# A fifth buffer for the split weights and one more half of lookahead in a decoder trunk on one core

## The chip, the core and the metric

The kernel runs on one core of a Trainium2 chip. The core has five engines, each with its own instruction queue that is worked off in order: TensorE (PE in the rows; its weight loads are PEld), VectorE (DVE), ScalarE (ACT), GpSimd (POOL) and SyncE (SP), which here issues nearly all the loads. The metric is the device time of one execution in microseconds; before the change it is 2073.59 us, the median of three runs.

## The reference

One sequence of 256 tokens with 2048 features goes through two layers in float32. Layer 0 mixes tokens by pooling, layer 1 by attention; each layer then has a gated feed-forward part (FFN) with 5632 inner features. A vector c gives every layer six modulation vectors.

```python
cond = silu(c)
for i in range(2):
    mod = cond @ w_ada[i] + b_ada[i]                  # 2048 -> 6 x 2048
    sh1, sc1, g1, sh2, sc2, g2 = split(mod, 6)
    h = rmsnorm(x, norm_g[i, 0]) * (1 + sc1) + sh1
    y = pool_mixer(h, pool_w, pool_scale) if i == 0 else moba_attention(h, w_qkv, w_o, rel_table)
    x = x + g1 * y
    h = rmsnorm(x, norm_g[i, 1]) * (1 + sc2) + sh2
    u = causal_conv3(h @ w_up[i], conv_w[i]) + conv_b[i]   # 2048 -> 2 x 5632
    val, gate = split(u, 2)
    x = x + g2 * ((silu(gate) * val) @ w_down[i])          # 5632 -> 2048
return rmsnorm(x, final_g)
```

With 256 tokens the attention has a single block, so every head attends causally to its own block with the relative bias. All weights are read once.

## The kernel before

**Split weights.** Activations lie feature by feature: 128 features on the partitions, 256 tokens along the row. Each float32 operand is split in two parts, hi (rounded to fp32r) and lo (the rest), and each product is made of three matmuls: hi x hi, hi x lo and lo x hi. The weights are used in *pieces* (`steps`) of 512 x 512, 1 MB, loaded by SyncE into one of five raw tiles (`RAW = 5`), in order. `w_use` (line 986) takes a piece in two *halves* of 128 x 1024: ScalarE copies the half to hi, VectorE subtracts hi from the raw half and writes lo. Both parts have a ring of `HB = 4` tiles of their own.

**Lookahead.** A half that is split is put on `pending`; only when more than `LAG = 2` halves wait there does `run_half` emit the matmuls of the oldest. So in program order the split of half n is followed by the matmuls of half n-2 and then by what belongs to it: the hooks of its piece (scores, norms), one or two entries of `tasks` (convolution, SiLU, residual additions), at most two `folds` and the `deferred` work. ScalarE and VectorE work in order, so a later split stands behind all this.

**Stages.** The *opening* computes modulation vectors of layer 0 out of w_ada in slices (tiles ws, sums accs, rows row on TensorE, columns mods), and the pooling mixer beside them; its loads are paced by raw tiles that come free. Then come FFN 0 (pieces uv, ug for w_up, d for w_down), attention (pieces k, q, v, wo; scores sc, softmax tiles sm) and FFN 1. The modulation of layer 1 is summed on VectorE beside the matmuls (tiles wa, sum acc, an accumulation of 128 x 2048 a time), and folded into columns by transposes (turn, cols). These accumulations are events of their own between two pieces (`ada_side`) and are not tied to `run_half`.

**What sets the order.** Up to event 200 (pieces up to about 90) a list scheduler orders each engine by its own estimate of times and the priorities in the code; from there on program order holds. The opening's first actions are the loads of c and x, the squares of x (sqx, into raw tiles), transposes of x to xT, and `cond` = SiLU(c) on ScalarE, before the first weight slice is used.

**Memory.** The pool lays its tiles one after another in SBUF: five raw tiles of 8192 bytes a partition, then four hi tiles, then four lo tiles. Each hi or lo tile is 1056 words long, of which words 16 to 1039 are used. `ones` is 128 x 128, of which column 0 is read (`slice_use`); `rel` holds the bias table.

Of the kernel before, what the change touches and what calls it, by code (L numbers as in the profile page):

```python
# [9 lines left out]
F32 = mybir.dt.float32  # L10
F32R = mybir.dt.float32r
# [6 lines left out]
P = 128  # L18
# [3 lines left out]
BUCKETS = 32  # L22
# [3 lines left out]
def bucket_starts():  # L26

    exact = BUCKETS // 2

    def bucket(n):  # L30
        if n < exact:
            return n
        big = exact + int(math.log(n / exact) / math.log(MAX_DIST / exact) * (BUCKETS - exact) + 1e-9)
        return min(big, BUCKETS - 1)

    of = [bucket(n) for n in range(4 * MAX_DIST)]
    return [next((n for n, b in enumerate(of) if b >= want), 1 << 20) for want in range(BUCKETS)]
# [19 lines left out]
def trunk(ctx: ExitStack, tc: tile.TileContext, x, c, norm_g, w_ada, b_ada, pool_w, pool_scale, w_qkv, w_o,  # L57
          rel_table, w_up, conv_w, conv_b, w_down, final_g, out):
    nc = tc.nc
    pe, ve, ac = (InOrder(tc, e) for e in (nc.tensor, nc.vector, nc.scalar))  # L60
    _, S, D = x.shape
# [4 lines left out]
    H = rel_table.shape[1]  # L66
    NT = S // P
    SCALE = float(P) ** -0.5
    C = 512
    S2 = 2 * S  # L70
    Q = 32

    const = ctx.enter_context(tc.tile_pool(name="const", bufs=1))
    wp = ctx.enter_context(tc.tile_pool(name="wp", bufs=1))
# [2 lines left out]
    dram = ctx.enter_context(tc.tile_pool(name="dram", bufs=1, space=bass.MemoryType.DRAM))  # L77

    PE_BLOCKS = ((2, 5, 8, 11, 14), (3, 7, 11, 15), (2, 4, 6, 9, 11, 13, 15), (2, 5, 7, 10, 13, 15), ())
    RAW, HB, LAG, T4, PRIO = 5, 4, 2, 6, 1000  # L80

    def raw_tile(name):
        return wp.tile([P, 4 * C], F32, tag="raw", name=name, bufs=RAW)
# [4 lines left out]
    def aux(name):  # L88
        return psum.tile([P, C], F32, tag="aux", name=name, bufs=2)

    def wt(shape, tag, bufs, name, dt=F32):
        return work.tile(shape, dt, tag=tag, bufs=bufs, name=name)


    ident = const.tile([P, P], F32, name="ident")
    make_identity(nc, ident)
    ones = const.tile([P, P], F32, name="ones")
    nc.gpsimd.memset(ones, 1.0)
    same = const.tile([P, P], F32, name="same")
    for q in range(4):  # L100
# [565 lines left out]
    def bias_rows():  # L666

        starts = bucket_starts() + [1 << 20]
        st = const.tile([P, BUCKETS + 1], F32, name="starts")
        for b, v in enumerate(starts):  # L670
            nc.gpsimd.memset(st[:, b:b + 1], float(v))
        rel = const.tile([BUCKETS, H + 8], F32, name="rel")[:, :H]
        nc.gpsimd.dma_start(rel, rel_table)
        e = wt([H, S + P], "t4", T4, "bias_e")
        nc.gpsimd.memset(e, NEG)
        for t in range(NT):
            ni = wt([P, 1], "st", 8, f"ni{t}", I32)
            nc.gpsimd.iota(ni, pattern=[[0, 1]], base=t * P, channel_multiplier=1)
            n = wt([P, 1], "st", 8, f"nf{t}")
            ve.tensor_copy(n, ni)  # L680
            ge = wt([P, BUCKETS + 1], "oh", 2, f"ge{t}")
            ve.tensor_scalar(ge, st, n, None, op0=ALU.is_le)
            oh = wt([P, BUCKETS + 1], "oh", 2, f"oh{t}")
            ve.tensor_tensor(oh[:, :BUCKETS], ge[:, :BUCKETS], ge[:, 1:], op=ALU.subtract)
            ps = aux(f"ohp{t}")
            pe.transpose(ps[:BUCKETS, :P], oh[:, :BUCKETS], ident)
            ohT = wt([BUCKETS, P], "vec", 4, f"ohT{t}")
            ve.tensor_copy(ohT, ps[:BUCKETS, :P])
            ps2 = aux(f"ohe{t}")
            pe.matmul(ps2[:H, :P], rel, ohT, start=True, stop=True)  # L690
            ve.tensor_copy(e[:, P - 1 + t * P:P - 1 + (t + 1) * P], ps2[:H, :P])
        nc.gpsimd.dma_start(bias_dram, e)
# [273 lines left out]
    def run_half():  # L966
        i, half, hi, lo = pending.pop(0)
        steps[i][3](half, hi, lo)
        if half == 1:
            for f in hooks.get(i, ()):  # L970
                f()
        h_next = ahead.pop(0) if ahead else None
        if h_next:
            h_next()
        else:
            run_tasks(2 if len(tasks) > MANY else 1)
        for _ in range(2):
            if folds:
                folds.pop(0)()
        for d in list(deferred):  # L980
            d[0] -= 1
            if d[0] <= 0:
                deferred.remove(d)
                d[1]()

    def w_use(i):
        def use(r):
            for half in range(2):

                hi, lo = (wp.tile([P, 2 * C + 32], F32R, tag=w, name=f"{w}{i}_{half}", bufs=HB)[:, 16:16 + 2 * C]  # L990
                          for w in ("hi", "lo"))
                src = r[:, half * 2 * C:(half + 1) * 2 * C]
                ac.activation(hi, src, AF.Copy)
                ve.tensor_tensor(lo, src, hi.bitcast(F32), op=ALU.subtract)
                pending.append((i, half) + tuple(t.rearrange("p (k c) -> p k c", k=2) for t in (hi, lo)))
                if len(pending) > LAG:
                    run_half()
        return use
# [47 lines left out]
    i = 0  # L1046
    for s in range(4):
        nxt = slices[s + 1] if s < 3 else []
        for g in range(FIRST):
            event(w_load(i), w_use(i))  # L1050
            i += 1
            if g == 0:
                at(len(events) - 1, lambda s=s: (slice_done(3, s, s > 0), h_blocks(0, 1, 4 * s, 4)))
            while nxt and (FIRST - SPARE) * (8 - len(nxt)) < 8 * (g + 1):
                event(*nxt.pop(0))
# [3 lines left out]
    while i < len(steps):  # L1059
        event(w_load(i), w_use(i))  # L1060
        i += 1
        if side:
            due = min(due + rates[steps[i - 1][0].tensor.name] + (LATE if side[0][:2] == (1, 5) else 0), 2.0)
        quiet = any(-PRE <= i - e < QUIET for e in ends) or i < START
        while side and due >= 1.0 and not quiet:
            due -= 1.0
            p = side.pop(0)
            event(ada_load(*p), ada_side(*p))
# [64 lines left out]
```

## Time and profile before

| | us |
|---|---|
| runs | 2073.27, 2073.59, 2078.25 |
| median of the runs | 2073.59 |
| the profiled execution | 2076.08 |
| its span | 2074.3 |
| TensorE busy in it | 2013.0 (97%) |
| VectorE busy | 1641.4 (79%) |
| ScalarE busy | 960.2 (46%) |

The span reaches from the first to the last instruction of the profiled execution; the rows further down are of that execution. A row of a timeline merges equal instructions that follow each other; the bracket at its end is the engine's idle time ahead of it and what ended it. TensorE's matmuls overlap, so a matmul's own duration is more than the time from its start to the next one's.

### The profile page before, as it was taken

Reading aid. Unit: us, or ns where it says so; the run is one execution under the profiler, and the core shown is the slowest. Engines: PE = TensorE matmul, PEld = TensorE weight load, DVE = VectorE, ACT = ScalarE, POOL = GpSimd, SP = SyncE. Lnnn points to the kernel's source line nnn. Section 1 sums busy time; section 2 is a strip of 40 time slices with the busy share of each in tenths; the row PEclk is TensorE's granted clock in tenths of the full one; section 3 lists DMA queues with packets and bytes.
Section 4 is the critical chain, followed back from the end, with each engine's and each line's share of the span. In section 5 each row is a group of like instructions: output and inputs, shape, how many; then the busy total and the mean of one; then the engine's idle time right before and its main releaser. Section 6 shows DMA issues by size and latency. Waiting matters only on the chain. (4 is left out here: it accounts for less than half of the span.)

```text
span 2074.3 us, 38497 instructions
## 1 busy us (share of the span) xinstructions
PE 2013.0 (97%) x16292; PEld 1907.9 (92%) x16292; DVE 1641.4 (79%) x2023; ACT 960.2 (46%) x1206; POOL 12.0 (1%) x64
## 2 busy tenths in 40 slices
PE   6898999999999999999999999999999999999998
PEld 2445999999999999999989889999999999999998
DVE  6887899899889999997787887879885666556666
ACT  3112534566454345444444444446543555435454
POOL 1000000000000000000000000000000000000000
PEclk8988999999999999999999999999999999999999
DMA  9998999655997989896888788678875555556551
GB/s 355 346 363 324 345 346 326 222 191 196 336 360 279 377 320 320 305 324 213 311 288 326 265 308 313 223 250 284 280 268 187 200 195 192 197 189 200 187 202 62
DMA packets 236445, 558.78 MB, mean 269 GB/s; under 512 B 9272, under 2 KB 9592, under 8 KB 221680
## 3 DMA queue, kind: packets, MB, share of 16 engines
q1 hardware_dynamic: 234800, 553.17, 75.4%
q8 instruction: 127, 2.08, 0.4%
q0 software_dynamic: 896, 2.49, 0.3%
q10 hardware_dynamic: 576, 0.67, 0.1%
q14 instruction: 46, 0.38, 0.0%
HBM read 554.17 MB, written 2.12 MB: 268 GB/s over the span
## 5 line engine op out<-in xcount | busy, mean ns | idle before, releaser
L50 DVE TENSOR_TENSOR lo<-w,hi 128x1024 fp32r<-128x1024 f32 x656 | 790.9, 1221 | 260.0 <-ACT hi L50 259.1
L50 ACT ACTIVATE hi<-w 128x1024 fp32r<-128x1024 f32 x656 | 683.2, 1059 | 630.5 <-PE d L50 185.6
L50 PE MATMUL uv<-h,hi 128*128 128x256 f32 x2816 | 485.1, 278 | 3.8 <-ACT h L50 3.8
L50 PE MATMUL d<-act,hi 128*128 128x256 f32 x2816 | 482.0, 277 | 0.6 <-ACT hi L50 0.6
L50 PE MATMUL ug<-h,hi 128*128 128x256 f32 x2816 | 481.8, 276 | 0.0
L50 PEld LDWEIGHTS uv<-h,hi 128*128 128x128 f32 x2816 | 426.6, 189 | 4.5 <-ACT h L50 4.1
L50 PEld LDWEIGHTS d<-act,hi 128*128 128x128 f32 x2816 | 424.9, 188 | 0.9 <-ACT hi L50 0.8
L50 PEld LDWEIGHTS ug<-h,hi 128*128 128x128 f32 x2816 | 424.0, 188 | 0.0
L50 PE MATMUL d<-act,lo 128*128 128x256 f32 x1408 | 387.4, 277 | 4.0 <-DVE lo L50 4.0
L50 PE MATMUL uv<-h,lo 128*128 128x256 f32 x1408 | 387.9, 277 | 0.0
L50 PE MATMUL ug<-h,lo 128*128 128x256 f32 x1408 | 386.3, 276 | 0.0
L50 PEld LDWEIGHTS d<-act,lo 128*128 128x128 f32 x1408 | 263.9, 188 | 4.8 <-DVE lo L50 4.8
L50 PEld LDWEIGHTS uv<-h,lo 128*128 128x128 f32 x1408 | 265.1, 189 | 0.0
L50 PEld LDWEIGHTS ug<-h,lo 128*128 128x128 f32 x1408 | 263.5, 188 | 0.0
L50 DVE SCALAR_TENSOR_TENSOR acc<-wa,cond,acc 128x2048 f32<-128x2048 f32 x105 | 246.3, 2346 | 6.6 <-DMA wa<-in_w_ada_dram 6.3
L50 DVE SCALAR_TENSOR_TENSOR accs<-ws,cond,accs 128x512 f32<-128x512 f32 (+1 forms) x179 | 157.4, 882 | 17.2 <-ACT accs L50 7.9
L50 PE MATMUL k<-h,hi 128*128 128x256 f32 x512 | 93.7, 285 | 1.1 <-ACT h L50 1.1
L50 PE MATMUL row<-ws,cond 128*1 128x512 f32 x152 | 81.5, 663 | 8.3 <-DMA ws<-in_w_ada_dram 8.3
L50 PE MATMUL q<-h,hi 128*128 128x256 f32 x512 | 88.7, 278 | 0.0
L50 PE MATMUL wo<-o,hi 128*128 128x256 f32 x512 | 88.3, 277 | 0.0
L50 PEld LDWEIGHTS k<-h,hi 128*128 128x128 f32 x512 | 80.1, 191 | 2.3 <-ACT h L50 1.4
L50 PE MATMUL v<-hi,h 128*128 128x512 f32 x256 | 80.1, 394 | 0.0
(157 smaller groups left out, 1753.9 us busy)
## 6 DMA issues: line engine op xcount, KB each, us to landing
w<-in_w_up_dram SPq DMA_DIRECT2D x176, 1024.0 KB, 5.1
wa<-in_w_ada_dram SPq DMA_DIRECT2D x112, 1024.0 KB, 5.8
w<-in_w_down_dram SPq DMA_DIRECT2D x88, 1024.0 KB, 5.1
ws<-in_w_ada_dram SPq DMA_DIRECT2D x56, 1024.0 KB, 7.6
w<-in_w_qkv_dram SPq DMA_DIRECT2D x48, 1024.0 KB, 6.4
ws<-in_w_ada_dram SPq DMA_DIRECT2D x48, 512.0 KB, 6.5
w<-in_w_o_dram SPq DMA_DIRECT2D x16, 1024.0 KB, 6.8
pw<-in_pool_w_dram SPq DMA_DIRECT2D x4, 1024.0 KB, 9.0
```

What stands on the lines that cost most here:

```text
L50: ins = call(*args, **kwargs)
```

## The change

Each part of the split weights gets five tiles in place of four, and `LAG` goes from 2 to 3, so that the matmuls of half n are emitted behind the split of half n+3. To make room the padding of these tiles goes, `ones` shrinks to 128 x 32, and `rel` moves to another pool and loses its padding. Between the hi and the lo tiles stands a tile `gap` of 512 bytes a partition, which is cleared once. The table of thresholds takes 48 columns in place of 33, of which 33 are used.

```diff
-    RAW, HB, LAG, T4, PRIO = 5, 4, 2, 6, 1000
+    RAW, HB, LAG, T4, PRIO = 5, 5, 3, 6, 1000
...
+    rel = wt([BUCKETS, H], "rel", 1, "rel")
...
-    ones = const.tile([P, P], F32, name="ones")
+    ones = const.tile([P, Q], F32, name="ones")
...
-        st = const.tile([P, BUCKETS + 1], F32, name="starts")
+        st = const.tile([P, 48], F32, name="starts")[:, :BUCKETS + 1]
...
-        rel = const.tile([BUCKETS, H + 8], F32, name="rel")[:, :H]
...
+    gap = []
+
     def w_use(i):
         def use(r):
             for half in range(2):
-
-                hi, lo = (wp.tile([P, 2 * C + 32], F32R, tag=w, name=f"{w}{i}_{half}", bufs=HB)[:, 16:16 + 2 * C]
-                          for w in ("hi", "lo"))
+                hi = wp.tile([P, 2 * C], F32R, tag="hi", name=f"hi{i}_{half}", bufs=HB)
+                if not gap:
+
+                    gap.append(wp.tile([P, P], F32, tag="gap", name="gap", bufs=1))
+                    nc.gpsimd.memset(gap[0], 0.0)
+                lo = wp.tile([P, 2 * C], F32R, tag="lo", name=f"lo{i}_{half}", bufs=HB)
```

The order of each engine changes with it. First pair: ScalarE at the very start, before and now. bT_r are the biases that are loaded for transposing, sqx the squares of x (x_90 and x_92 before, x_91 and x_93 now), xps a transposed piece of x.

```order
L123 DMA bT_r_108<-in_b_ada_dram 96x128
L50 ACT_TABLE_LOAD
L50 ACTIVATE cond<-cT 128x16
L123 DMA bT_r_108<-in_b_ada_dram 32x128
L123 DMA bT_r_111<-in_b_ada_dram 64x128
L50 ACTIVATE sqx_118,ms_117<-x_90 128x2048
L50 ACTIVATE sqx_120,ms_117<-x_92 128x2048
L50 ACTIVATE xT<-xps_135 128x512
```

```order
L125 DMA bT_r_109<-in_b_ada_dram 96x128
L125 DMA bT_r_109<-in_b_ada_dram 32x128
L125 DMA bT_r_112<-in_b_ada_dram 64x128
L50 ACT_TABLE_LOAD
L50 ACTIVATE sqx_119,ms_118<-x_91 128x2048
L50 ACT_TABLE_LOAD
L50 ACTIVATE cond<-cT 128x16
L50 ACTIVATE sqx_121,ms_118<-x_93 128x2048
L50 ACTIVATE xT<-xps_136 128x512
```

The table load and cond stood ahead of the last two loads of biases; now all three loads come first, one square stands ahead of cond, and there is a second table load.

Second pair: VectorE in the attention, at the v piece 155 of the second group of heads, before and now. sm0_1 and sm1_1 are the softmax tiles of its two row blocks of tokens, sc1_1 scores that TensorE has just made, acc1_4 a sum of the modulation of layer 1.

```order
L50 TENSOR_TENSOR lo154_1_11285<-w154_11139,hi154_1_11284 128x1024
L50 TENSOR_TENSOR sm1_1_11300<-sc1_1_0_11301,bias1_11247 128x512
L50 TENSOR_TENSOR sm1_1_11300<-sc1_1_2_11305,bias1_11247 128x512
L50 TENSOR_REDUCE mx1_1_11309<-sm1_1_11300 128x4
L50 RECIPROCAL ri0_1_11312<-su0_1_11258 128x4
L50 TENSOR_SCALAR sm0_1_11249<-sm0_1_11249,ri0_1_11312 128x128 x4
L50 SCALAR_TENSOR_TENSOR acc1_4_10992<-wa1_4_4_11208,cond_94,acc1_4_10992 128x2048
L50 TENSOR_TENSOR lo155_0_11324<-w155_11211,hi155_0_11323 128x1024
```

```order
L50 TENSOR_TENSOR lo154_1_11271<-w154_11115,hi154_1_11270 128x1024
L50 SCALAR_TENSOR_TENSOR acc1_4_10957<-wa1_4_4_11157,cond_95,acc1_4_10957 128x2048
L50 TENSOR_TENSOR lo155_0_11296<-w155_11160,hi155_0_11295 128x1024
L50 TENSOR_TENSOR sm1_1_11311<-sc1_1_0_11312,bias1_11258 128x512
L50 TENSOR_TENSOR sm1_1_11311<-sc1_1_2_11316,bias1_11258 128x512
L50 TENSOR_REDUCE mx1_1_11320<-sm1_1_11311 128x4
L50 RECIPROCAL ri0_1_11323<-su0_1_11269 128x4
L50 TENSOR_SCALAR sm0_1_11260<-sm0_1_11260,ri0_1_11323 128x128 x4
L50 TENSOR_TENSOR lo155_1_11330<-w155_11160,hi155_1_11329 128x1024
```

The half lo155_0 stood behind the work on the scores and now stands ahead of it; the accumulation stays ahead of lo155_0.

Third pair: VectorE in FFN 0 at piece 84, the first down-projection's second part. dy0 to dy3 are results of the down-projection that wait to be added to the residual xT once their gate vector is known.

```order
L50 SCALAR_TENSOR_TENSOR xT_100<-dy0_5533,mod_113,xT_100 128x256 x4
L50 SCALAR_TENSOR_TENSOR xT_100<-dy1_5597,mod_113,xT_100 128x256 x4
L50 SCALAR_TENSOR_TENSOR xT_100<-dy2_5661,mod_113,xT_100 128x256 x4
L50 SCALAR_TENSOR_TENSOR xT_100<-dy3_5913,mod_113,xT_100 128x256 x2
L50 TENSOR_TENSOR lo84_0_6672<-w84_6525,hi84_0_6671 128x1024
```

```order
L50 SCALAR_TENSOR_TENSOR xT_101<-dy0_5544,mod_114,xT_101 128x256 x4
L50 SCALAR_TENSOR_TENSOR xT_101<-dy1_5608,mod_114,xT_101 128x256 x4
L50 SCALAR_TENSOR_TENSOR xT_101<-dy2_5672,mod_114,xT_101 128x256
L50 TENSOR_TENSOR lo84_0_6646<-w84_6500,hi84_0_6645 128x1024
L50 SCALAR_TENSOR_TENSOR xT_101<-dy2_5672,mod_114,xT_101 128x256
L50 TENSOR_TENSOR lo84_1_6678<-w84_6500,hi84_1_6677 128x1024
```

Fourteen additions stood ahead of lo84_0, now nine; both halves of the piece now stand among them.

## Rows read from the trace of the kernel before

**Rows 1.** Page, part 1: busy us, share of the span, instructions.
```profile
PE 2013.0 (97%) x16292; PEld 1907.9 (92%) x16292; DVE 1641.4 (79%) x2023; ACT 960.2 (46%) x1206; POOL 12.0 (1%) x64
```
**Rows 2.** Stretches: length, PE, PEld, DVE, ACT, POOL busy (instructions), PEclk, DMA share, GB/s.
```profile
100.00:200.00 100.00, 91.26 (x343) 44.53 (x341) 74.77 (x134) 18.88 (x30) 0.67 (x2) 0.88 0.91 337
...
1500.00:1600.00 100.00, 100.00 (x884) 100.00 (x884) 70.58 (x87) 41.78 (x42) 0.00 (x0) 1.00 0.69 237
```
**Rows 3.** Waits of PE: us in total, times, longest us.
```profile
PE d L50 <- DVE lo L50: 4.0, 3, 1.9
...
PE v L50 <- DVE lo L50: 2.5, 3, 0.8
PE k L50 <- DVE lo L50: 2.1, 4, 1.2
...
PE d L50 <- ACT hi L50: 0.6, 1, 0.6
```
**Rows 4.** Timeline of PE at 883 us: start, us, instruction, idle before.
```profile
882.80 0.39 PE L50 MATMUL d<-act,hi 128*128 128x256 f32 x2
883.02 0.28 PE L50 MATMUL d<-act,lo 128*128 128x256 f32 x1
883.14 0.39 PE L50 MATMUL d<-act,hi 128*128 128x256 f32 x2
885.40 0.46 PE L50 MATMUL d<-act,lo 128*128 128x256 f32 x1 [1.87 <-DVE lo L50]
```
**Rows 5.** Stretches with the columns of Rows 2.
```profile
885.60:889.00 3.40, 3.40 (x17) 3.40 (x17) 3.40 (x3) 0.00 (x0) 0.00 (x0) 0.50 1.01 335
...
206.00:940.00 734.00, 728.23 (x6392) 727.02 (x6391) 668.08 (x781) 364.55 (x435) 0.79 (x1) 1.00 0.85 303
...
866.00:932.00 66.00, 64.09 (x549) 63.70 (x548) 63.53 (x83) 32.91 (x37) 0.00 (x0) 0.97 0.86 306
```
**Rows 6.** Timeline of DVE in the attention's second group of heads.
```profile
1080.85 2.35 DVE L50 SCALAR_TENSOR_TENSOR acc<-wa,cond,acc 128x2048 f32<-128x2048 f32 x1
1083.11 2.36 DVE L50 TENSOR_TENSOR lo<-w,hi 128x1024 fp32r<-128x1024 f32 x2
```
**Rows 7.** Timeline of DVE around 668 us.
```profile
662.47 5.63 DVE L50 SCALAR_TENSOR_TENSOR xT<-dy,mod,xT 128x256 f32<-128x256 f32 x14
668.00 1.22 DVE L50 TENSOR_TENSOR lo<-w,hi 128x1024 fp32r<-128x1024 f32 x1
```
**Rows 8.** Timeline of ACT at the start of the program.
```profile
7.04 1.28 ACT L50 ACT_TABLE_LOAD   x1 [7.04 <-DMA x<-in_x_dram]
8.34 0.22 ACT L50 ACTIVATE cond<-cT 128x16 f32<-128x16 f32 x1
8.87 0.89 ACTq L123 DMA_DIRECT2D bT_r<-in_b_ada_dram  x2
9.80 1.91 ACT L50 ACTIVATE sqx<-x 128x2048 f32<-128x2048 f32 x1 [1.25 <-DMA x<-in_x_dram]
...
13.60 1.06 ACT L50 ACTIVATE xT<-xps 128x512 f32<-128x512 f32 x2
```
**Rows 9.** Timeline of DVE: the first accumulations over weight slices.
```profile
25.93 12.19 DVE L50 SCALAR_TENSOR_TENSOR accs<-ws,cond,accs 128x512 f32<-128x512 f32 x16 [2.19 <-ACT accs L50]
```
**Rows 10.** Waits of the SP queue: us in total, times, longest us.
```profile
SPq L251 <- DVE accs L50: 104.2, 44, 9.4
```
**Rows 11.** Stretches of 5 us with the columns of Rows 2.
```profile
25.00:30.00 5.00, 2.06 (x4) 0.17 (x4) 3.89 (x6) 2.21 (x4) 0.00 (x0) 0.88 0.76 261
30.00:35.00 5.00, 1.11 (x2) 0.00 (x0) 4.86 (x7) 0.00 (x0) 0.00 (x0) 0.50 1.05 395
```
**Rows 12.** Groups by line and shape, DVE and then ACT: count, busy us, mean ns, idle.
```profile
L50 DVE TENSOR_TENSOR lo<-w,hi 128x1024 fp32r<-128x1024 f32 x656 | 790.9, 1221 | 260.0 <-ACT hi L50 259.1
...
L50 DVE TENSOR_TENSOR val<-gate,val 128x1024 f32<-128x1024 f32 x22 | 26.9, 1224 | 3.4 <-ACT gate L50 3.0
...
L50 ACT ACTIVATE hi<-w 128x1024 fp32r<-128x1024 f32 x656 | 683.2, 1059 | 630.5 <-PE d L50 185.6 <-PE ug L50 152.3 <-PE uv L50 141.9
...
L50 ACT ACTIVATE gate<-gate 128x1024 f32<-128x1024 f32 x22 | 23.3, 1059 | 13.7 <-DVE gate L50 13.6
```

## The prediction

> **What bounds the kernel now.** I read the page first, then the engines by stretches of 100 us, then TensorE's waits, and last the timelines around the waits. TensorE is busy 97% of the span [rows 1]. From about 206 us on it runs without a pause nearly everywhere: 1500 to 1600 us holds 884 matmuls and no idle time, so one matmul starts every 113 ns, and a half of a piece (4 feature blocks x 2 row blocks x 3 products = 24 matmuls) takes 2.72 us [rows 2]. Nothing in this change shortens a matmul. The opening, up to 206 us, is another regime: the DMA engines are busy 0.91 of 100 to 200 us, TensorE issues 343 matmuls, and its mean granted clock is 0.88 [rows 2]. So the change can act in two places: on the pauses of the long part, and on the opening.
>
> **The pauses that belong to this change.** TensorE waits for a split weight half in eleven places after 206 us: d for lo 4.0 us in three waits, v for lo 2.5 us in three, k for lo 2.1 us in four, d for hi 0.6 us in one, together 9.2 us [rows 3]. Idle time undercounts a pause, because a matmul's modelled end (0.28 us after its start) lies after the start of the next. At 883 us a lo matmul normally starts 0.22 us after the pair of hi matmuls ahead of it; after the pause it starts 2.26 us after its pair, so 2.04 us were lost where 1.87 us of idle time stand [rows 4]. That is 0.17 us a wait, 1.9 us for eleven: 11.1 us. Behind that pause the clock falls from 2.4 to 1.2 GHz for 3.4 us (0.50 granted, 17 matmuls) [rows 5], which costs half of it, 1.7 us. All that the edit of the buffers could give back is therefore 12.8 us: 3.2 around 668 us (two lo waits of together 2.1 us, the one hi wait, 0.5 us of undercount), 3.7 at 883 us, 3.0 in the three v waits, 2.8 in the four k waits.
>
> **What three halves ahead removes.** In the second pair of rows in the section on the change, VectorE takes the half lo155_0 after two bias additions, a maximum, four scalings and an accumulation (acc, 2.3 us). Those additions wait for TensorE's scores, and lo stands behind all of it in order; it begins at 1083.11 us, behind an acc that begins at 1080.85 us [rows 6]. With the change the same lo stands ahead of the additions. A task of half n then follows the lo of half n+3 and not of half n+2, so TensorE has one more half, 2.72 us, before it misses the next. The three v waits cost 1.0 us each, so they go: -3.0. Of the k waits, two are behind such a chain and go; the other two are behind a row of transposes and reductions on VectorE that folds an accumulation, and I leave 0.5 us there: -2.3.
>
> The other two bursts have a VectorE that is full and not one that waits: 63.53 us busy of the 66 from 866 to 932 us [rows 5]. There a half ahead is worth less than 2.72 us, since the same work has still to be done. What VectorE has done more when the burst begins is one lo, 1.14 us from start to start [rows 6], and what moves behind the late lo is the task work that stood just ahead of it. At 883 us that is one product (val, 1.22 us): 2.3 us together. The accumulation over the next mixer's weights stays ahead of lo, as it is written at the load's place and not at the half's. So the 2.04 us go, the fall of the clock behind them probably too, but VectorE stays full to 932 us and takes some back: I take -2.3 of 3.7. At 668 us fourteen residual additions stand ahead of lo84_0 in one row of 5.63 us [rows 7]; in the new order nine do (third pair of rows). TensorE's new order also asks for that half earlier, so I take -2.0 of 3.2. Sum: -(3.0 + 2.3 + 2.3 + 2.0) = -9.6 us.
>
> The Trainium skill (Perfetto Trace Analysis, Identifying Performance Opportunities) says that consistent bubbles, the same gap over and over on the engine that should be saturated, can mean that buffers have run out. Here the gaps are few and unlike, so by that rule buffers are not short and the term would be 0; that case is among the rivals.
>
> **What the opening costs.** The change renames and moves tiles, and the scheduler orders the opening by its own estimates, so ScalarE's first rows change (first pair of rows). Now: two loads of biases are issued until 9.76 us, the table load and cond are already behind, and the squares begin at 9.80 us and lead to the first xT copy at 13.60 us, 3.80 us later [rows 8]. Before cond there was an idle engine, so its table load of 1.28 us and cond's 0.22 us delayed nothing. In the new order these stand behind the loads: table load, first square, a second table load, cond, second square. The xT copy then starts at 9.80 + 1.28 + 3.80 + 1.28 + 0.22 = 16.38 us, 2.8 us later. That has no cover. The rest of ScalarE's chain follows in order, and VectorE's first accumulation, at 25.93 us, waits for the ScalarE accumulation ahead of it [rows 9]; that accumulation frees the first weight tile, and the SyncE queue waits up to 9.4 us for it [rows 10]. The DMA engines already run dry there: 0.76 busy from 25 to 30 us, where every full stretch shows over 1.0 [rows 11]. As the opening is bound by DMA, I add all of it: +2.8 us. Bounds: 0, if a later hole swallows it; 5.6, if the shift moves as much again into a stretch of the lower clock.
>
> On the table load the Trainium skill (ScalarE: Activation LUTs, What ACT_TABLE_LOAD costs) counts a drain of 1380 ns beside the 1283 ns. In the trace cond starts 0.02 us after its table load ends, so no drain follows it [rows 8]; with the page's figure the term would be an estimated 4.2 us and the sum 1.4 us worse.
>
> **The rest.** Of the table of ones the kernel reads one column only, and the moved table rel is loaded once: 0. The memset of the gap has the shape that the ones had, whose own shrinks: 0. The parts lose their 128-byte padding. The pool lays the tiles in a row, so raw and hi tiles were 64 bytes off a multiple of 4096 and now are on it; hi and lo of one half lie 20,992 bytes apart instead of 16,896, both 512 above a multiple of 4096. A product of two tiles that lie multiples of 4096 bytes apart (gate and val) takes 1224 ns, the same shape in lo 1221; the activation in place on gate 1059 ns, hi 1059 [rows 12]. So I take no change of any duration.
>
> **Sum.** 2076.08 (the profiled execution, 1.8 above its span) - 9.6 + 2.8 = 2069.3 us. That execution lies 2.5 us above the median of the runs, 2073.59; carried over: **2066.8 us**.
>
> **Rivals.** (a) The shift of the opening is absorbed, as it has holes of its own, and the bursts clear fully: 2073.59 - 12.8 = 2060.8, or about 2063 with one of the two. For it: the DMA engines are at 0.91 between 100 and 200 us, not full. Against it: the first hole is caused by the very chain that gets longer.
> (b) VectorE is the bound in its bursts and takes back all at 668 and 883 us; only the waits on scores go: 2073.59 - 5.3 + 2.8 = 2071.1. For it: 63.53 of 66 us busy [rows 5]. By the rule of the Trainium skill above (Perfetto Trace Analysis) nothing at all goes, and the opening alone would give 2076.4; the trace agrees only in that no gap repeats on a beat. Both are no change by measurement.
> (c) Slower: the equal addresses of raw and hi make the two-input lo longer on VectorE. From 206 to 940 us VectorE is idle 734 - 668 = 66 us [rows 5], that is 0.24 us for each of 270 halves. Up to a lo of 1.46 us nothing shows; a quarter longer (+0.305 us) costs 270 x 0.065 = 17.5 us, 2084.3. Against it: the equal durations of [rows 12], where both inputs lay as raw and hi now do.
>
> **Chances.** The forecast, 2063.5 to 2069, 0.46, of which 0.36 lies below 2067.4; (a) 0.18; (b) 0.27; (c) 0.09. What counts as a change is 0.3%, 6.2 us, about what a measurement of this kernel can tell: faster below 2067.4, slower above 2079.8. Faster 0.36 + 0.18 = 0.54, same 0.10 + 0.27 = 0.37, slower 0.09. The range of 8 in 10 goes from all of (a), 2060.5, to just under the case in which the opening alone counts, 2075.5.
>
> **What would show it.** Right: no wait of v for lo, the k waits under 1 us, no stretch at the lower clock near 885 us; ScalarE's first xT copy near 16.4 us and two table loads ahead of it; the first accumulation on VectorE near 28.7 us; 113 ns between matmuls and lo at 1.22 us as now. Wrong: waits for lo in the same places, TensorE reaching its steady stretch at 206 us or before, or any duration of lo, hi or a matmul that differs.

## The result, and the profile after

The changed kernel takes 2124.38 us, the median of four runs (2121.93 to 2126.78), beside 2074.77 us for the kernel before: a ratio of 1.0237, 95% interval 1.0224 to 1.0249. It is slower by 50 us. The prediction said 2066.8 us, and its range ended at 2075.5 us.

The profiled execution is 50.3 us longer in its span (2124.6 against 2074.3 us). The page's busy times of the engines after, in us, answer [rows 1]:

```profile
PE 2068.7 (97%) x16292; PEld 1966.7 (93%) x16292; DVE 1643.4 (77%) x2023; ACT 960.3 (45%) x1207; POOL 12.1 (1%) x65
```

VectorE and ScalarE do the same work in the same time. TensorE has the same 16292 instructions and is busy 55.7 us longer. The groups by line and shape say the same of the splits (count, busy us, mean ns, idle):

```profile
L50 DVE TENSOR_TENSOR lo<-w,hi 128x1024 fp32r<-128x1024 f32 x656 | 794.2, 1222 | 319.3 <-ACT hi L50 317.6
L50 ACT ACTIVATE hi<-w 128x1024 fp32r<-128x1024 f32 x656 | 682.4, 1056 | 673.3 <-PE d L50 214.7
```

1222 and 1056 ns stand where 1221 and 1059 ns stood [rows 12]. The stretches of the changed kernel (columns of [rows 2]) show the difference:

```profile
300.00:400.00 100.00, 100.00 (x854) 100.00 (x853) 88.08 (x107) 39.26 (x44) 0.00 (x0) 1.00 0.85 296
1500.00:1600.00 100.00, 100.00 (x851) 100.00 (x850) 74.77 (x88) 45.28 (x49) 0.00 (x0) 1.00 0.70 243
```

In them TensorE waits for nothing, its granted clock is 1.00 (2.4 GHz), and it has 851 matmuls in 100 us where it had 884 [rows 2]. From start to start that is 117.8 ns on average and not 113.3. (A stretch also counts the matmuls that only reach into it, so 100 us divided by its count comes out up to 0.4 ns low.) The timeline of TensorE in the changed kernel at 1500 us (start, us, instruction) shows three matmuls at this pace:

```profile
1500.40 0.40 PE L50 MATMUL uv<-h,hi 128*128 128x256 f32 x2
1500.63 0.28 PE L50 MATMUL uv<-h,lo 128*128 128x256 f32 x1
1500.75 0.40 PE L50 MATMUL uv<-h,hi 128*128 128x256 f32 x2
```

Three matmuls take 0.35 us from start to start; in the kernel before they take 0.34 [rows 4]. The waits for the split weights are gone. Of TensorE's waits only these do not lie in the opening, and they are the norms' (us in total, times, longest; of the two of uv one ends the opening):

```profile
PE uv L50 <- ACT h L50: 3.9, 2, 2.7
...
PE rrow L50 <- DVE st_r L50: 2.6, 2, 1.3
...
PE k L50 <- ACT h L50: 1.1, 1, 1.1
```

For every matmul of 128x128 weights against 256 columns I took the time from its start to the next start, from 210 us on. Two groups stand apart: 111 to 114 ns (called **fast** from here on), and 115 to 121 ns (**slow**). The kernel before has 13,652 matmuls at the fast pace and 1,141 at the slow one, the changed kernel 88 and 14,768. So the slow pace is not new: the kernel before has it too, in short spells.

**Sum.** 13,627 more slow matmuls at 4.44 ns (100 us / 851 less 100 us / 884) are +60.5 us. The pauses, which the prediction put at 12.8 us, are gone, all of them: -12.8. The long part starts later: the 40th matmul of the FFN starts at 211.5 us and not at 208.6: +2.9. Together +50.6 us; the spans differ by 50.3.

### The profile page after: what moved, and what is told of

It reads as the page before. It is cut to its first block, busy times and chain, and to the rows that moved or that the text cites. A ratio compares the mean times of both kernels' runs of the same rounds, so it can differ in the third digit from the quotient of the medians.

```text
span 2124.6 us, 38506 instructions
## 1 busy us (share of the span) xinstructions
PE 2068.7 (97%) x16292; PEld 1966.7 (93%) x16292; DVE 1643.4 (77%) x2023; ACT 960.3 (45%) x1207; POOL 12.1 (1%) x65
## 4 chain that ended last, share of the span: by engine, by line
PE 95%; DVE 2%; DMA 1%; ACT 1%; issue 1%; ACTq 0%; SPq 0%; DVEq 0%
PE uv L50 24%; PE ug L50 23%; PE d L50 23%; PE k L50 4%; PE q L50 4%; PE wo L50 4%; PE v L50 4%; PE row L50 2%; PE pp L50 2%; PE mods L50 1%; DMA ws<-in_w_ada_dram 1%; DVE accs L50 1%; DVE pool_room L50 1%; PE sc L50 0%; PE po L50 0%
## 5 line engine op out<-in xcount | busy, mean ns | idle before, releaser
L50 DVE TENSOR_TENSOR lo<-w,hi 128x1024 fp32r<-128x1024 f32 x656 | 794.2, 1222 | 319.3 <-ACT hi L50 317.6
L50 ACT ACTIVATE hi<-w 128x1024 fp32r<-128x1024 f32 x656 | 682.4, 1056 | 673.3 <-PE d L50 214.7
L50 PE MATMUL uv<-h,hi 128*128 128x256 f32 x2816 | 504.0, 281 | 3.9 <-ACT h L50 3.9
L50 PE MATMUL ug<-h,hi 128*128 128x256 f32 x2816 | 500.7, 279 | 0.0
L50 PE MATMUL d<-act,hi 128*128 128x256 f32 x2816 | 497.5, 279 | 0.0
L50 PEld LDWEIGHTS uv<-h,hi 128*128 128x128 f32 x2816 | 433.6, 189 | 4.5 <-ACT h L50 4.1
L50 PEld LDWEIGHTS ug<-h,hi 128*128 128x128 f32 x2816 | 430.9, 188 | 0.0
L50 PEld LDWEIGHTS d<-act,hi 128*128 128x128 f32 x2816 | 429.2, 187 | 0.0
L50 PE MATMUL uv<-h,lo 128*128 128x256 f32 x1408 | 395.2, 281 | 0.0
L50 PE MATMUL ug<-h,lo 128*128 128x256 f32 x1408 | 393.9, 280 | 0.0
```

The lines of the kernel that those rows point to most:

```text
L50: ins = call(*args, **kwargs)
```

## The experiments

Times are medians, ratios are to the kernel before, run beside it. "Place" is the distance from the start of h, or of act, up to the start of a split tile, modulo 256 bytes. TensorE loads hi or lo as weights and streams h or act past them, so these are the two operands of its matmuls (for v they change parts). In all kernels but the two alternating ones further down, h and act start at the same address modulo 256, so a tile has one place.

**One: what of the change slows TensorE.** Four kernels, each with a part of the change.

```diff
-    RAW, HB, LAG, T4, PRIO = 5, 5, 3, 6, 1000
+    RAW, HB, LAG, T4, PRIO = 5, 5, 2, 6, 1000
```

> The changed kernel with LAG back at 2: its five tiles of each part and its addresses stay, only the order of the instructions is that of two halves of lookahead. From 206 us on the changed kernel starts a matmul every 117.5 ns (851 per 100 us) where the kernel before starts one every 113.06 ns (884). Theory A (the moving operands h and act have left the multiples of 1024 bytes on which they lay): 117.5 ns stays, 2124 us or a few more, since the waits for lo come back, 2124 to 2135. Theory B (the split tiles now all lie at one address modulo 4096, where the padded ones were 128 bytes apart): the same, 2124 to 2135. Theory C (the new order starts TensorE in another rhythm, and with the waits gone nothing takes it out of it): 884 per 100 us again, about 2074 us.

Measured: 2137.00 us, ratio 1.0303 (1.0280 to 1.0327). Its stretch:

```profile
1500.00:1600.00 100.00, 100.00 (x851) 100.00 (x851) 76.68 (x90) 46.21 (x52) 0.00 (x0) 1.00 0.72 253
```

The slow pace is there with the old lookahead: theory C falls. The waits are back, the same for v and k as [rows 3], less for d (us in total, times, longest):

```profile
PE v L50 <- DVE lo L50: 2.5, 3, 0.8
PE k L50 <- DVE lo L50: 2.1, 4, 1.2
PE d L50 <- DVE lo L50: 1.1, 1, 1.1
```

At equal addresses, then, one more half of lookahead gains 8.5 us by the spans (2133.1 to 2124.6) and 12.6 us by the medians. Of the 4.6 us of d waits [rows 3] only 1.1 are left here with the old lookahead, so the slower pace or the fifth tile had already taken most of those.

```diff
-                hi, lo = (wp.tile([P, 2 * C + 32], F32R, tag=w, name=f"{w}{i}_{half}", bufs=HB)[:, 16:16 + 2 * C]
+                hi, lo = (wp.tile([P, 2 * C], F32R, tag=w, name=f"{w}{i}_{half}", bufs=HB)
```

> The kernel before with only the padding of the hi and lo tiles gone: four tiles of each, each part at one address modulo 4096, LAG 2, h and act still on multiples of 1024 bytes, no gap tile. Theory A (moving operands off their multiples of 1024 bytes): 884 matmuls per 100 us, 2074 us. Theory B (split tiles at one address modulo 4096): 851 per 100 us, 2124 to 2135 us. Theory C (order): 2074 us.

Measured: 2163.00 us, ratio 1.0429 (1.0405 to 1.0452), with this stretch:

```profile
1500.00:1600.00 100.00, 100.00 (x836) 100.00 (x835) 82.71 (x94) 48.66 (x55) 0.00 (x0) 1.00 0.75 260
```

Slower still than the changed kernel, 120.0 ns a matmul from start to start, by the padding alone. This speaks against theories A and C; B had the sign but not a third pace.

```diff
-    ones = const.tile([P, P], F32, name="ones")
+    ones = const.tile([P, Q], F32, name="ones")
```

> The kernel before with only the table of ones at 128 x 32 in place of 128 x 128: everything behind it in memory moves down by 384 bytes, so that h lies 640 bytes above a multiple of 1024 (as in the changed kernel) and act 640 (there 128); padding, four tiles and LAG 2 as before. Theory A (moving operands): 851 per 100 us, 2124 to 2135 us. Theory B (split tiles at one address modulo 4096; here they are not): 884, 2074 us. Theory C (order): 2074 us.

Measured: 2073.87 us, ratio 0.9999 (0.9986 to 1.0013), 885 matmuls from 1500 to 1600 us. Moving all tiles together changes nothing; h has left its multiple of 1024 without harm. Theory A falls.

```diff
-    ones = const.tile([P, Q], F32, name="ones")
+    ones = const.tile([P, P], F32, name="ones")
...
-                    gap.append(wp.tile([P, P], F32, tag="gap", name="gap", bufs=1))
-                    nc.gpsimd.memset(gap[0], 0.0)
...
```

> The changed kernel with its five tiles and LAG 3, but the full table of ones and no gap tile: h and act lie on multiples of 1024 bytes again, as in the kernel before; the split tiles still lie at one address modulo 4096 each. Theory A (moving operands): 884 per 100 us, no waits for lo, so that what the prediction worked out for the waits shows, 2060 to 2070 us. Theory B (split tiles at one address): 851 per 100 us, 2124 us. Theory C (order): 851, 2124 us.

Measured: 2122.19 us, ratio 1.0226 (1.0202 to 1.0250), 851 matmuls from 1500 to 1600 us. The gap tile and the table of ones are not the cause. Theory B is left. But the four runs fit another reading as well: the place is 192 in the changed kernel, in the one with LAG 2 and in this one, 0 without padding, and in the two fast kernels 64 for half of the tiles and 192 for the other half.

**Two: equal addresses, or the place?** The edits move tiles by a few columns. The first of these is the last kernel with

```diff
-        st = const.tile([P, 48], F32, name="starts")[:, :BUCKETS + 1]
+        st = const.tile([P, 80], F32, name="starts")[:, :BUCKETS + 1]
...
-    rel = wt([BUCKETS, H], "rel", 1, "rel")
+    rel = wt([BUCKETS, H + 32], "rel", 1, "rel")[:, :H]
```

> The changed kernel (five tiles, LAG 3, full table of ones, no gap tile) with 128 bytes added ahead of the raw tiles and 128 ahead of act: hi and lo now lie 64 bytes above a multiple of 256 as counted from h and from act; in the changed kernel, in the one with LAG 2 and in the one with h and act back on multiples of 1024 they lay 64 below one, in the kernel before 64 above or 64 below by turns, and without padding exactly on one (836 matmuls per 100 us). All tiles of a part still lie at one address modulo 4096. Theory B (one address modulo 4096 for all tiles of a part makes TensorE slow): 851 per 100 us, 2120 us. Theory D (what counts is the distance from the weights to the moving operand modulo 256): 884 per 100 us, no waits for lo, 2060 to 2070 us.

Measured: 2081.05 us, ratio 1.0034 (1.0015 to 1.0054). Neither theory holds as it stood. Two stretches of the same execution:

```profile
300.00:400.00 100.00, 100.00 (x853) 100.00 (x852) 87.75 (x106) 38.96 (x43) 0.00 (x0) 1.00 0.86 295
...
1800.00:1900.00 100.00, 100.00 (x885) 100.00 (x884) 54.49 (x61) 40.45 (x41) 0.00 (x0) 1.00 0.58 195
```

With all tiles at place 64, TensorE is slow from 209 to 673 us, over 3,889 matmuls and all five tiles, and fast from 1349 to 2048 us. The pace is a rhythm that holds itself: 9,604 matmuls are fast, 5,237 slow. It turns only where other work, or a pause, comes between the matmuls: in no run whose tiles all lie at place 64, or all at 192, does the pace turn inside an unbroken row of these matmuls (six of one pace ahead, six of the other behind). TensorE's timeline of this run at 673 us shows the turn just behind two matmuls that fold columns (modc):

```profile
672.00 0.40 PE L50 MATMUL d<-act,hi 128*128 128x256 f32 x2
672.23 0.28 PE L50 MATMUL d<-act,lo 128*128 128x256 f32 x1
672.35 0.33 PE L50 MATMUL modc<-cols,same 128*128 128x64 f32 x2
...
673.29 0.39 PE L50 MATMUL d<-act,hi 128*128 128x256 f32 x2
673.51 0.28 PE L50 MATMUL d<-act,lo 128*128 128x256 f32 x1
```

Ahead of it a pair of hi takes 0.23 us from its start to the lo behind it, after it 0.22, which is all that can be seen at two decimals; the counts above are from the trace's nanoseconds.

The next two are the kernel without padding, moved by a wider `rel` (H + 24, and H + 40, in place of H + 8) and by a pad tile ahead of act (48 and 32 columns).

```diff
-        rel = const.tile([BUCKETS, H + 8], F32, name="rel")[:, :H]
+        rel = const.tile([BUCKETS, H + 24], F32, name="rel")[:, :H]
...
+    pad = wt([P, 48], "pad", 1, "pad")
+    nc.gpsimd.memset(pad, 0.0)
```

> The kernel before without padding (four tiles, LAG 2, one address modulo 4096 for each part), moved up by 64 bytes as counted from h and act. Without the move it took 2163 us at 836 per 100 us. Theory B (one address modulo 4096): 836 per 100 us, 2163 us. Theory D (distance to the moving operand modulo 256): 884 per 100 us, 2074 us.

Measured: 2093.68 us, ratio 1.0094 (1.0074 to 1.0114). The kernel without padding at place 64 in place of 0 gains 69 us; it too has both rhythms for hundreds of us, 7,976 fast and 6,788 slow.

> The same moved up by 128 bytes as counted from h and act. Theory B (one address modulo 4096): 836 per 100 us, 2163 us. Theory D (distance to the moving operand modulo 256) says only that the rate may be another than at 0, 64 or 192; if what counts is modulo 128, it is 836 per 100 us as at 0.

Measured: 2149.14 us, ratio 1.0361 (1.0339 to 1.0384).

```profile
1500.00:1600.00 100.00, 100.00 (x835) 100.00 (x835) 77.38 (x86) 46.94 (x51) 0.00 (x0) 1.00 0.74 255
1800.00:1900.00 100.00, 100.00 (x845) 100.00 (x844) 54.10 (x59) 42.72 (x46) 0.00 (x0) 1.00 0.54 187
```

Places 0 and 128 give 835 to 845; the fast rhythm does not appear at either (10 and 19 fast matmuls in all). At place 128 the times from start to start are spread from 115 to 123 ns, 119.0 on average; at place 0 nearly all are 120.

```diff
-                hi, lo = (wp.tile([P, 2 * C + 32], F32R, tag=w, name=f"{w}{i}_{half}", bufs=HB)[:, 16:16 + 2 * C]
+                hi, lo = (wp.tile([P, 2 * C + 64], F32R, tag=w, name=f"{w}{i}_{half}", bufs=HB)[:, 48:48 + 2 * C]
```

> The kernel before with its four tiles of each part 4352 bytes apart in place of 4224, the weights 192 bytes into each: no two tiles of a part at one address modulo 4096, but all of them 64 below a multiple of 256 as counted from h and act. LAG 2, table of ones and all else as before. Theory B (one address modulo 4096): 884 per 100 us, 2074 us. Theory D (distance to the moving operand modulo 256): 851 per 100 us in the long part, 2124 to 2140 us.

Measured: 2129.94 us, ratio 1.0269 (1.0236 to 1.0301). Padding and unequal addresses modulo 4096, and still slow: theory B falls. The stretches again show both rhythms:

```profile
700.00:780.00 80.00, 80.00 (x709) 80.00 (x708) 74.05 (x77) 31.83 (x32) 0.00 (x0) 1.00 0.95 359
800.00:900.00 100.00, 100.00 (x851) 100.00 (x851) 90.15 (x95) 50.67 (x59) 0.00 (x0) 1.00 0.88 311
```

709 matmuls in 80 us are the fast pace; at place 192 it lasts here from 696 to 784 us and is seldom reached. So theory E: at 64 modulo 128 there are two rhythms, and a ring whose tiles all lie at one place modulo 256 does not leave the slow one by itself. What the padding of the kernel before did was to put tiles 128 bytes apart modulo 256. Its trace shows where the slow rhythm ends; here on TensorE, where a half at place 192 (ug) gives way to one at place 64 (uv):

```profile
372.40 0.40 PE L50 MATMUL ug<-h,hi 128*128 128x256 f32 x2
372.64 0.28 PE L50 MATMUL ug<-h,lo 128*128 128x256 f32 x1
372.75 0.39 PE L50 MATMUL uv<-h,hi 128*128 128x256 f32 x2
372.98 0.28 PE L50 MATMUL uv<-h,lo 128*128 128x256 f32 x1
373.09 0.39 PE L50 MATMUL uv<-h,hi 128*128 128x256 f32 x2
```

The first two triples start 0.35 us apart, the next two (372.75, 373.09) 0.34. Inside unbroken rows of matmuls (six of one pace, then six of the other) the kernel before has six turns from slow to fast, all at a step from place 192 to 64, and none from fast to slow.

**Three: a ring of five that alternates.** The tiles lie in pairs hi, lo, with 128 bytes behind each pair, and are used in turn. In place of the lines for hi, gap and lo of the changed kernel stands:

```diff
...
+                k = (2 * i + half) % HB
+                hi = wp.tile([P, 2 * C], F32R, tag=f"hi{k}", name=f"hi{i}_{half}", bufs=1)
+                lo = wp.tile([P, 2 * C], F32R, tag=f"lo{k}", name=f"lo{i}_{half}", bufs=1)
+                if len(gap) < HB:
+                    gap.append(wp.tile([P, Q], F32, tag=f"gap{k}", name=f"gap{k}", bufs=1))
+                    nc.gpsimd.memset(gap[-1], 0.0)
...
```

> The changed kernel with five tiles of each part and LAG 3, but laid in pairs hi, lo with a gap of 128 bytes between the pairs, and used in turn, so that successive halves lie by turns 64 above and 64 below a multiple of 256 as counted from h and act, as the tiles of the kernel before do. Theory E (at 64 modulo 128 TensorE has two rhythms, 113 and 117.5 ns a matmul; with all tiles at one place modulo 256 it stays in whichever it is in, and a ring whose tiles lie by turns at 64 and 192 brings it back to 113 ns in a few us): over 90% of the matmuls at 113 ns, no waits for lo, so the 12.8 us of waits of the kernel before show as a gain, 2058 to 2066 us. Theory F (five tiles and LAG 3 in themselves bring the slow rhythm): mostly 117.5 ns, about 2120 us.

Measured: 2065.78 us (11 runs), ratio 0.9956 (0.9943 to 0.9970): 0.4% faster than the kernel before, with an interval that leaves out 1. 13,238 matmuls are fast and 1,609 slow; of TensorE's waits for weights one of 0.6 us is left:

```profile
PE k L50 <- ACT h L50: 1.1, 1, 1.1
PE d L50 <- ACT hi L50: 0.6, 1, 0.6
```

Theory F falls. All 19 turns from slow to fast inside unbroken rows lie at a step from 192 to 64. This version also turns the other way in such rows, ten times, and all ten lie where TensorE changes from h to act or back; one of them:

```profile
1505.03 0.39 PE L50 MATMUL ug<-h,hi 128*128 128x256 f32 x2
1505.26 0.28 PE L50 MATMUL ug<-h,lo 128*128 128x256 f32 x1
1505.37 0.40 PE L50 MATMUL d<-act,hi 128*128 128x256 f32 x2
1505.60 0.28 PE L50 MATMUL d<-act,lo 128*128 128x256 f32 x1
1505.72 0.40 PE L50 MATMUL d<-act,hi 128*128 128x256 f32 x2
```

The five gaps put act 640 bytes further from h, 128 modulo 256: a tile at place 64 from h is at 192 from act. So the place repeats at eight of these ten changes. The repeat alone does not do it: within one operand it comes over 200 times in the fast pace, as a ring of five must, and the pace goes on. The change of operand alone does not do it either: in the kernel before, where h and act lie alike, twelve such changes come in the fast pace and none ends it. The slow spells behind the ten turns hold 664 matmuls, an estimated 2.9 us at 4.44 ns each.

The same without the gaps, so that all pairs lie at place 192 from both h and act:

```diff
...
-                if len(gap) < HB:
-                    gap.append(wp.tile([P, Q], F32, tag=f"gap{k}", name=f"gap{k}", bufs=1))
-                    nc.gpsimd.memset(gap[-1], 0.0)
```

> The same without the gaps between the pairs: all five pairs lie 64 below a multiple of 256 as counted from h and act, nothing else differs. Theory E: the slow rhythm that TensorE enters at the end of the opening stays, 851 matmuls per 100 us in most of the long part, 2105 to 2127 us. If pairs or the turn of the tiles were what helped in the version with gaps, this one is as fast, 2058 to 2066 us.

Measured: 2124.83 us, ratio 1.0237 (1.0207 to 1.0268), 66 matmuls at the fast pace and 14,747 at the slow one. 128 bytes behind each pair are worth 59 us.

```profile
1500.00:1600.00 100.00, 100.00 (x852) 100.00 (x851) 72.17 (x83) 43.33 (x47) 0.00 (x0) 1.00 0.67 238
```

**Four: is the fifth tile needed?** The kernel before with

```diff
-    RAW, HB, LAG, T4, PRIO = 5, 4, 2, 6, 1000
+    RAW, HB, LAG, T4, PRIO = 5, 4, 3, 6, 1000
```

> The kernel before with LAG 3 and nothing else: four padded tiles of each part, the split of the half three ahead ahead of the matmuls. Theory E: the tiles still lie by turns at 64 and 192 modulo 256, so 113 ns; and if the lookahead alone takes the waits away, no wait for lo: 2058 to 2066 us. If the fifth tile is what the waits need (a split of half n+4 must wait for the matmuls of half n), waits for hi or lo stay or come up on ScalarE: 2070 us or more.

Measured: 2076.03 us (12 runs), ratio 1.0000 (0.9990 to 1.0010). The pace is fast. The waits have moved. Behind 206 us TensorE has these, beside three of the norms that it had before (us in total, times, longest):

```profile
PE ms L50 <- ACT sq L50: 5.5, 2, 2.8
...
PE d L50 <- DVE gate L50: 3.5, 2, 2.1
...
PE d L50 <- DVE lo L50: 0.8, 1, 0.8
```

The timelines of ScalarE (two rows) and of VectorE (two rows) ahead of one of the first kind show where it comes from (start, us, instruction, idle before):

```profile
933.98 1.06 ACT L50 ACTIVATE hi<-w 128x1024 fp32r<-128x1024 f32 x1 [3.64 <-PE d L50]
937.12 1.24 ACT L50 ACTIVATE sq<-xT 128x512 f32<-128x512 f32 x3 [2.08 <-DVE xT L50]
...
935.07 1.23 DVE L50 TENSOR_TENSOR lo<-w,hi 128x1024 fp32r<-128x1024 f32 x1 [2.97 <-ACT hi L50]
936.22 1.65 DVE L50 SCALAR_TENSOR_TENSOR xT<-d,mod,xT 128x256 f32<-128x256 f32 x4
```

With four tiles, the split three ahead must wait until TensorE lets go of the tile: hi starts on ScalarE behind 3.64 us of idle time, lo on VectorE waits for it, xT stands behind lo in order, and the norm's squares wait for xT. In all, 9.8 us of waits stand here where 9.2 us of waits for hi and lo stood [rows 3]. The waits for gate were not followed up.

**Five: the opening.** The alternating version without the clearing of the gaps (`memset` taken out).

> The version with five tiles, LAG 3 and gaps of 128 bytes between the pairs, but the gaps are not cleared. Without that work for GpSimd the scheduler's order of the opening on ScalarE is that of the kernel before again (cond ahead of the squares, one table load), so that the first xT copy starts at 13.6 us and not at 16.3 us, and the first accumulation on VectorE at 25.9 us and not at 28.2 us. If those 2.8 us reach the end of the opening, as the prediction has it, this version takes 2062 to 2064 us where the one that clears the gaps took 2065.8 us, and its long part starts some 3 us earlier (the 40th matmul of the FFN at about 209 us, there 211.9 us). If the opening, bound by its DMAs, absorbs them, it takes 2065 to 2067 us, the same start within a microsecond. The rhythm of 113 ns stays in over 85% of the matmuls by either.

Measured: 2066.75 us, ratio 0.9965 (0.9951 to 0.9978). ScalarE has its old order and its old times:

```profile
6.99 1.28 ACT L50 ACT_TABLE_LOAD   x1 [6.99 <-DMA x<-in_x_dram]
8.29 0.22 ACT L50 ACTIVATE cond<-cT 128x16 f32<-128x16 f32 x1
...
13.64 1.06 ACT L50 ACTIVATE xT<-xps 128x512 f32<-128x512 f32 x2
```

The 40th matmul of the FFN still starts at 211.5 us; with the clearing it is 211.9. The 2.7 us on ScalarE are absorbed before the opening ends, as the second reading of the expectation has it.

## Why the prediction was wrong

**The pace of TensorE: the step that failed.** "So I take no change of any duration", under "The rest". I had the new addresses, and priced them at VectorE's and ScalarE's splits, where [rows 12] gives them the right answer: 1222 and 1056 ns. The operation that reads both the weights and h or act, some 15,000 times, was covered only by "Nothing in this change shortens a matmul". It left open the other direction. Rival (c) had the right sign on the wrong engine: equal addresses on VectorE, up to 2084.3. The term that was put at nothing is +60.5 us. The trace of before had the warning, had I not taken the mean of 113 ns for the only pace there is: 1,141 matmuls at 115 to 121 ns, mostly in the attention, and turns from one pace to the other at a change of tile.

The Trainium skill (SBUF — State Buffer, A bandwidth-pool intuition that's wrong) gives TensorE a second, independent read port for its weights. Read by itself that gives the two operands' addresses no say; the runs here, at 835 to 885 matmuls in 100 us by where the tiles lie, do not agree with such a reading for this stream. They do not show that the ports are to blame.

**The waits: right in kind.** All v and k waits went. At 668 and 883 us the changed kernel has no pause and no fall of the clock, but its TensorE is slower there and asks later, so this run alone does not show what the lookahead does in the two bursts. The alternating version shows it: at the fast pace one wait of 0.6 us is left. I had taken -9.6 of 12.8; there it is about -12. The doubt that a full VectorE takes time back at both bursts (rival b) fell.

That version came to 2065.78 us, beside a forecast of 2066.8. The closeness is in part luck. The kernel before measured 2076.17 us beside it, so it gained 10.4 us, and 7.2 in the version without the clearing, where the forecast was a gain of 6.8. By the spans (2066.6 against 2074.3) it is 7.7 us, of which about -12 for the waits, +3.3 for a long part that starts later (40th matmul at 211.9 and not at 208.6) and +2.1 for 468 more slow matmuls make -6.6.

The rule on consistent bubbles that the prediction weighed (the Trainium skill, Perfetto Trace Analysis, Identifying Performance Opportunities) speaks of a gap that repeats. It does not say that buffers suffice where gaps are few and unlike, as the prediction read it, and here they did not.

**Three halves ahead, five tiles.** The prediction argued with the order on VectorE only. The run with four tiles showed that the fifth is a condition, and not room to spare: ratio 1.0000.

**The opening: right on ScalarE, wrong on its price.** Forecast were a first xT copy at 16.38 us behind a second table load, and a first accumulation at 28.7 us. These are ScalarE's rows and VectorE's row of the changed kernel:

```profile
13.13 1.28 ACT L50 ACT_TABLE_LOAD   x1
14.43 0.22 ACT L50 ACTIVATE cond<-cT 128x16 f32<-128x16 f32 x1
...
16.44 1.06 ACT L50 ACTIVATE xT<-xps 128x512 f32<-128x512 f32 x2
```

```profile
28.78 1.54 DVE L50 SCALAR_TENSOR_TENSOR accs<-ws,cond,accs 128x512 f32<-128x512 f32 x2 [2.18 <-ACT accs L50]
```

But "that has no cover" was wrong: the alternating versions with and without this shift (first xT copy at 16.33 and 13.64 us) start the long part within 0.4 us and take the same time within their spread. It was the clearing of the gap tile, work for GpSimd, that moved the order. The long part does start 2.9 us later than before, close to the +2.8 of the sum, but that is luck as far as these runs show: the versions with ScalarE's old order start at 211.8 (full table of ones, no gap) and 211.5 us, the others with the old order anywhere from 203.7 to 212.8. What sets this start was not tried.

**What stays open.** Why the place matters to TensorE, and why the step from 192 to 64 ends the slow rhythm, is not shown: the runs show the dependence, not the mechanism. In every run h and act start at a multiple of 128 bytes, so the difference between 0 or 128 and 64 or 192 could as well go by the weights' own address; a run with h and act moved by 64 bytes would tell. The difference between 64 and 192 does not go by it alone: in the changed kernel and in the run at place 64 the split tiles start alike, 64 above a multiple of 256, and only h and act lie differently. That a change of operand starts slow spells where h and act lie 128 bytes apart rests on ten turns in the trace of the alternating version, and on the same ten in that of the version without the clearing; a version with act moved back by 128 bytes was not tried.

## What to carry to other kernels

When an edit moves tiles, list the addresses of the operands that the bounding engine reads, before and after, and compare the pace of that engine in a stretch without waits (matmuls per 100 us): here 4.4 ns on each of nearly 14,000 matmuls outweighed every wait for a split weight (60.5 us against 12.8). Padding that looks like waste may set that pace; take it out in a run of its own. And a deeper lookahead may need a deeper ring: here, without the fifth tile, the wait only moved to the engines that fill it.

## What the runs showed of the hardware

TensorE's pace at the full granted clock, for 128x128 weights against 256 columns of fp32r, goes by where the two operands start in SBUF. At a distance of 0 or 128 modulo 256 bytes it is 120.0 or 119.0 ns a matmul on average (835 to 845 in a stretch of 100 us). At 64 or 192 it is 113.3 or 117.8 ns (885 or 851). The last two are rhythms that each hold themselves over hundreds of us: at 64 both were seen at length, at 192 nearly always the slow one (in four of five kernels under 1% of the matmuls were fast, in the fifth 6%). A ring of tiles with both places finds back to the fast one at a step from 192 to 64; in the alternating version the spells behind its ten turns last 5 to 11 us.
